# Seven products for eight: the last feed-forward output of a decoder trunk in two recursive units

## The chip, the core and the metric

The kernel runs on one core of a Trainium2 chip. The metric is the device time of one launch in microseconds, as the median of three runs. Times inside an execution come from one profiled execution.

## The reference, cut to what matters

Two layers; each is a feed-forward block, a token mixer and a second feed-forward block on 512 tokens of width 1024. The change touches only the output projection of the very last feed-forward block.

```python
D_MODEL, SEQ, D_FF, DEPTH = 1024, 512, 2816, 2

def swiglu(x, w_in, w_out):
    gate, up = jnp.split(x @ w_in, 2, axis=-1)
    return (jax.nn.silu(gate) * up) @ w_out

for l in range(DEPTH):
    ...
    hn = rms_norm(h, g_ffn2[l]) * (1.0 + sc3) + sh3
    h = h + 0.5 * (1.0 + gt3) * swiglu(hn, w_ffn2_in[l], w_ffn2_out[l])
return h
```

## The kernel before, in words

Everything is held transposed: a tile has 128 features on the partitions and the 512 tokens along the free dimension. The residual stream is `h[0]` to `h[7]`, eight blocks of 128 of the 1024 features; two neighbours share one buffer, so that a listing names them in pairs (`h_85` is blocks 0 and 1, `h_91` blocks 6 and 7). The 2816 inner features of a feed-forward block are 22 blocks, `xs[0]` to `xs[21]`.

Every large float32 product is made from three matmuls. `split` turns an operand into a rounded high part (a cast on ACT, L141: `wH`, `actH`, `comH`) and a low part (a subtraction on DVE, L143: `wL`, `actL`, `comL`); `mm3` (L129 to L131) and `prod` (L433 to L435) then add wH x xH, wH x xL and wL x xH in PSUM. A weight block goes HBM, `wraw` (SP's queue), `wH` and `wL`. The pairs `wH`/`wL` are a ring of four buffers and `wraw` a ring of two, so a cast waits for the matmuls that used the pair four places earlier.

`ffn` works in two groups, `GROUPS = ((0, 12), (12, 22))`. For a group it first makes the inner blocks and then multiplies them by their rows of `w_out` and adds the result, times a gate `cg`, to `h`. The inner blocks are made two at a time by `pair_in`, which already uses a recursion with seven products: `pD`, `pF`, `pG` are PSUM tiles, each product is 24 matmuls of 256 columns (two output blocks, four contraction blocks, three matmuls), and sums of weight blocks are made partly by DMA (`raw` loads a block, `plus` is a second load on POOL's queue that accumulates into it) and partly by DVE (L375). The sums of inputs (`comH`, `comL` with the names P1, P2, T3, T4) are made once by `combine` and serve all pairs. The product with T4 of a pair is put off (`waiting`, `flush`) behind the first products of the next pair.

The output of a group is classical. For each output block i one PSUM tile `ps_mm` collects ten blocks x three matmuls of 512 columns, with the weights of a row in two halves of five blocks (128x640, L304), and `residual` (L343, DVE) adds it to `h[i]`. The last two output blocks, 6 and 7, are done in two halves of the tokens. In the last feed-forward block nothing follows (`ss` is None), so this second group's output, 240 matmuls of 512 columns' worth, is the end of the program; SP then stores each `h[i]` (L1510).

The framework orders the instructions of each engine when the program is built; each engine then works its row off in that order, and a row that waits holds up all rows behind it on its engine.

## Time and profile before

| | |
|---|---|
| median of three runs | 1797.73 us (1796.48 to 1798.9) |
| the profiled execution: time, span | 1801.11 us, 1799.3 us |
| granted TensorE clock | 0.997 |
| PE, DVE, ACT, POOL busy | 98%, 75%, 47%, 8% of the span |
| last pair of inner blocks ends, last output stage begins | 1743.25 us |
| last row of DVE begins | 1795.70 us |

In the rows of the profile the first number is a start in us from the span's beginning, the second the duration; then engine, line, operation, output and inputs, shape; a bracket at the end gives the engine's idle time before the row and what ended it. PEld is the weight load of a matmul; SPq is SP's queue of loads and stores.

### The profile page before, as it was taken

Reading aid. Unit: us, or ns where it says so; the run is one execution under the profiler, and the core shown is the slowest. Engines: PE = TensorE matmul, PEld = TensorE weight load, DVE = VectorE, ACT = ScalarE, POOL = GpSimd, SP = SyncE. Lnnn points to the kernel's source line nnn. Section 1 sums busy time; section 2 is a strip of 40 time slices with the busy share of each in tenths; the row PEclk is TensorE's granted clock in tenths of the full one; section 3 lists DMA queues with packets and bytes.
Section 4 is the critical chain, followed back from the end, with each engine's and each line's share of the span. In section 5 each row is a group of like instructions: output and inputs, shape, how many; then the busy total and the mean of one; then the engine's idle time right before and its main releaser. Section 6 shows DMA issues by size and latency. Waiting matters only on the chain.

```text
span 1799.3 us, 33746 instructions
## 1 busy us (share of the span) xinstructions
PE 1771.5 (98%) x13868; PEld 1616.9 (90%) x13868; DVE 1348.5 (75%) x2175; ACT 844.9 (47%) x1314; POOL 141.4 (8%) x225
## 2 busy tenths in 40 slices
PE   9999999999999999999999999999999999999999
PEld 7898999987778999899899989999876798999998
DVE  7877678777768877677888776887686788865862
ACT  7452355365444554255355515544644345523541
POOL 0101011000000011100100020010000000010000
PEclk9999999999999999999999999999999999999999
DMA  9667877522133676867737697773420427675742
GB/s 378 220 182 260 229 197 214 178 87 79 51 110 103 179 189 219 253 198 203 243 98 203 173 299 195 206 230 102 117 72 28 142 80 205 183 240 135 199 141 71
DMA packets 92267, 309.92 MB, mean 172 GB/s; under 512 B 10512, under 2 KB 11280, under 8 KB 91088
## 3 DMA queue, kind: packets, MB, share of 16 engines
q1 hardware_dynamic: 63072, 202.63, 33.3%
q0 software_dynamic: 29040, 105.13, 23.3%
q8 instruction: 109, 1.79, 0.4%
q14 instruction: 46, 0.38, 0.1%
HBM read 303.79 MB, written 3.93 MB: 171 GB/s over the span
## 4 chain that ended last, share of the span: by engine, by line
PE 84%; DVE 7%; DMA 3%; ACT 3%; issue 3%; POOL 0%; SPq 0%; ACTq 0%; POOLq 0%; DVEq 0%
PE ps_mm L129 14%; PE ps_mm L130 14%; PE ps_mm L131 14%; PE ps_d L433 7%; PE ps_d L435 7%; PE ps_d L434 7%; PE ps_f L435 3%; PE ps_f L433 3%; PE ps_f L434 3%; PE ps_g L435 2%; PE ps_g L433 2%; PE ps_g L434 2%; PE ps_mm L1410 1%; DVE wL L143 1%; DMA wada<-in_wa 1%
## 5 line engine op out<-in xcount | busy, mean ns | idle before, releaser
L141 ACT CAST wH<-wraw 128x1024 fp32r<-128x1024 f32 (+2 forms) x288 | 261.6, 915 | 463.0 <-PE ps_mm L130 198.0
L143 DVE TENSOR_TENSOR wL<-wraw,wH 128x1024 fp32r<-128x1024 f32 (+2 forms) x288 | 303.7, 1058 | 121.5 <-ACT wH L141 120.1
L129 PE MATMUL ps_mm<-actH,wH 128*128 128x512 f32 (+1 forms) x784 | 281.6, 359 | 1.9 <-ACT wH L141 1.9
L131 PE MATMUL ps_mm<-actH,wL 128*128 128x512 f32 (+1 forms) x784 | 281.2, 359 | 0.3 <-DVE wL L143 0.3
L130 PE MATMUL ps_mm<-actL,wH 128*128 128x512 f32 (+1 forms) x784 | 281.0, 358 | 0.0
L129 PE MATMUL ps_mm<-hnH,wH 128*128 128x512 f32 (+1 forms) x712 | 249.6, 356 | 2.9 <-ACT hnH L291 2.6
L130 PE MATMUL ps_mm<-hnL,wH 128*128 128x512 f32 (+1 forms) x712 | 247.1, 349 | 0.3
L131 PE MATMUL ps_mm<-hnH,wL 128*128 128x512 f32 (+1 forms) x712 | 246.1, 347 | 0.6 <-DVE wL L143 0.6
L433 PE MATMUL ps_d<-comH,wH 128*128 128x256 f32 x816 | 225.7, 277 | 0.0
L435 PE MATMUL ps_d<-comH,wL 128*128 128x256 f32 x816 | 224.9, 276 | 0.0
L434 PE MATMUL ps_d<-comL,wH 128*128 128x256 f32 x816 | 224.9, 276 | 0.0
L143 DVE TENSOR_TENSOR wL<-sum,wH 128x1024 fp32r<-128x1024 f32 x102 | 125.0, 1226 | 85.5 <-ACT wH L141 85.4
L199 DVE SCALAR_TENSOR_TENSOR wada<-wada,crep 128x1024 f32<-128x1024 f32 x128 | 153.7, 1222 | 31.5 <-DMA wada<-in_wadaT 31.1
L129 PEld LDWEIGHTS ps_mm<-actH,wH 128*128 128x128 f32 x784 | 149.1, 190 | 18.5 <-ACT wH L141 2.4
L131 PEld LDWEIGHTS ps_mm<-actH,wL 128*128 128x128 f32 x784 | 149.1, 190 | 17.4 <-DVE wL L143 1.1
L130 PEld LDWEIGHTS ps_mm<-actL,wH 128*128 128x128 f32 x784 | 149.1, 190 | 16.2
L433 PEld LDWEIGHTS ps_d<-comH,wH 128*128 128x128 f32 x816 | 157.0, 192 | 1.6 <-ACT s L459 1.6
L435 PEld LDWEIGHTS ps_d<-comH,wL 128*128 128x128 f32 x816 | 157.0, 192 | 0.0
L434 PEld LDWEIGHTS ps_d<-comL,wH 128*128 128x128 f32 x816 | 157.0, 192 | 0.0
L141 ACT CAST wH<-sum 128x1024 fp32r<-128x1024 f32 x102 | 106.9, 1048 | 106.4 <-PE ps_f L434 42.4
L129 PEld LDWEIGHTS ps_mm<-hnH,wH 128*128 128x128 f32 x712 | 135.0, 192 | 23.2 <-issue 7.6
L131 PEld LDWEIGHTS ps_mm<-hnH,wL 128*128 128x128 f32 x712 | 136.6, 192 | 13.7 <-DVE wL L143 1.0
(385 smaller groups left out, 3865.0 us busy)
## 6 DMA issues: line engine op xcount, KB each, us to landing
wada<-in_wadaT POOLq DMA_DIRECT2D x126, 512.0 KB, 4.8
wraw<-in_wmi SPq DMA_DIRECT2D x40, 512.0 KB, 3.5
wraw<-in_w2p SPq DMA_DIRECT2D x36, 512.0 KB, 4.1
wraw<-in_w1p SPq DMA_DIRECT2D x32, 512.0 KB, 4.7
wraw<-in_w1o SPq DMA_DIRECT2D x32, 384.0 KB, 4.9
wraw<-in_w2o SPq DMA_DIRECT2D x32, 384.0 KB, 4.2
wraw<-in_w1o SPq DMA_DIRECT2D x32, 320.0 KB, 3.6
wraw<-in_w2o SPq DMA_DIRECT2D x32, 320.0 KB, 3.4
```

Source lines behind the costliest of these rows:

```text
L129: mm(acc, wH, xH, start=start, stop=False)
L130: mm(acc, wH, xL, start=False, stop=False)
L131: latest["large"] = mm(acc, wL, xH, start=False, stop=stop)
L141: latest["cast"] = nc.scalar.copy(hi, src)
L143: return nc.vector.tensor_sub(lo, src, hi.bitcast(F32))
L199: stt(w, w, 1.0, crep, ALU.mult, ALU.mult, accum_out=out_)
L433: mm(acc, wH, xH, start=start and i + k == 0, stop=False, skip_group_check=True)
L434: mm(acc, wH, xL, start=False, stop=False, skip_group_check=True)
L435: mm(acc, wL, xH, start=False, stop=k == 3, skip_group_check=True)
L1410: latest["large"] = pin("PE", mm(paired(pts[n]), w, x, start=first, stop=last, skip_group_check=True))
```

## The change

In the last feed-forward block, the second group's output goes through a new function `strassen_out`. Eight of its ten inner blocks (12 to 19) are the contraction of a recursion with seven products; blocks 20 and 21 stay classical (`rest_rows`: eight output blocks x two blocks x three matmuls of 512 columns). There are two units, u = 0 and 1, each for four output blocks: g picks two of the four, kh four of the eight contraction blocks. Each unit has seven products of 24 matmuls of 256 columns.

- The sums of inputs P1, P2, T3, T4 are made by `gather` from `actH` and `actL`, four or six steps of 128x512 where `combine` needed two, and split like a weight. P1 is made ahead of unit 0; P2, T3 and T4 between unit 0's products; unit 1 uses them again.
- The sums of weights are made as in `pair_in`, with plain loads and accumulating loads, each now in two pieces of 128x512. Unit 0's first sum `S` takes the buffer `sum0` that the last pair used.
- The products' results reach `h` by `rows_to`, on halves of the tokens.
- The last two blocks of `h` are stored in halves.

```diff
@@ -360,7 +360,7 @@
             com = {n: tuple(ap_.tile([P, 4, H2], F32R, name=x, tag="com", bufs=8) for x in ("comH", "comL")) for n in ("P1", "P2", "T3", "T4")}
             n_first = 2 if first is None else 4
             tiles = (t for t in projector([w_in[l, j, g] for j in range(2 * n_first) for g in range(2)], hn, BANKS[:3], first, 1, ready) if t is not None)
-            xs, waiting, done, after, second = {}, [], [None], [None], [None]
+            xs, Xs, waiting, done, after, second = {}, {}, [], [None], [None], [None]
             def flush():
                 for f in waiting:
@@ -387,6 +387,7 @@
             def new_x(p):
                 X = tuple(ap_.tile([P, 2, T], F32R, name=x, tag="act", bufs=12) for x in ("actH", "actL"))
+                Xs[p] = X
                 for i in range(2):
                     xs[2 * p + i] = tuple(x[:, i] for x in X)
                 return X
@@ -485,6 +486,109 @@
                 waiting.append(rest)
+            def strassen_out(j0, j1):
+
+                kc = j0 + 8
+                full = lambda X, n, sl: X[n][:, :, sl].bitcast(F32)
+                new = {n: tuple(ap_.tile([P, 4, H2], F32R, name=x, tag="com", bufs=8) for x in ("comH", "comL")) for n in ("P1", "P2", "T3", "T4")}
+                q1 = ap_.tile([P, 4, H2], F32, name="q", tag="crep", bufs=1)
+                q2, q3 = (ap_.tile([P, 4, H2], F32, name="q", tag="act", bufs=12) for _ in range(2))
+
+                def gather(name):
+                    for n in range(2):
+                        x1, x2, c = Xs[j0 // 2 + n], Xs[j0 // 2 + 2 + n], slice(2 * n, 2 * n + 2)
+                        if name == "P1":
+                            tt(q1[:, c], full(x1, 0, lo_), full(x1, 0, hi_), ALU.subtract)
+                            tt(q1[:, c], q1[:, c], full(x1, 1, lo_), ALU.add)
+                            tt(q1[:, c], q1[:, c], full(x1, 1, hi_), ALU.subtract)
+                        elif name == "T3":
+                            tt(q3[:, c], full(x2, 0, hi_), full(x1, 0, hi_), ALU.subtract)
+                            tt(q3[:, c], q3[:, c], full(x2, 1, hi_), ALU.add)
+                            tt(q3[:, c], q3[:, c], full(x1, 1, hi_), ALU.subtract)
+                        else:
+                            q, sl = (q1, hi_) if name == "P2" else (q2, lo_)
+                            stt(q2[:, c], q[:, c], -1.0, full(x2, 0, sl), ALU.mult, ALU.subtract)
+                            tt(q2[:, c], q2[:, c], full(x2, 1, sl), ALU.subtract)
+                    split(*new[name], {"P1": q1, "T3": q3}.get(name, q2))
+                    return [tuple(t[:, k] for t in new[name]) for k in range(4)]
+
+                B11, B21, B22 = ([tuple(t[:, sl] for t in xs[k0 + k]) for k in range(4)] for k0, sl in ((j0, lo_), (j0 + 4, lo_), (j0 + 4, hi_)))
+                ncg = small_.tile([P, KD], F32, name="ncg", tag="gmod")
+                ts(ncg, cg, -1.0, None, ALU.mult)
+                flat = lambda t: t.rearrange("p i (b a) -> p i b a", b=2)
+                half_ = lambda n: E(n).rearrange("p (i t) -> p i t", i=2)
+
+                def parts(u, g, kh):
+                    return [(slice(4 * e, 4 * e + 4), w_out[l, 4 * u + 2 * g + e, :, j0 + 4 * kh : j0 + 4 * kh + 4]) for e in range(2)]
+
+                def raw_(srcs, tag=None):
+                    w = (ap_.tile if tag else wp.tile)([P, KD, P], F32, name=tag or "wraw", tag=tag or "wraw", bufs=1 if tag else 2)
+                    for c, s in srcs:
+                        nc.sync.dma_start(w[:, c], s)
+                    return w
+
+                def add_(w, srcs):
+                    for c, s in srcs:
+                        nc.gpsimd.dma_start(w[:, c], s, accum_op=ALU.add)
+
+                def rows_to(i0, gate, sl, x, woven=False):
+
+                    for i in range(2):
+                        hs = h[i0 + i][:, sl]
+                        if woven:
+                            hs = inorder(hs)
+                        stt(hs, x[:, i], gate[:, i0 + i : i0 + i + 1], hs, ALU.mult, ALU.add)
+
+                def rest_rows(u):
+                    w = hl(raw_([(slice(2 * i, 2 * i + 2), w_out[l, 4 * u + i, :, kc:j1]) for i in range(4)]))
+                    for i in range(4):
+                        pt = psum([P, T], "ps_mm", "x")
+                        for k in range(2):
+                            mm3(pt, tuple(t[:, 2 * i : 2 * i + 2] for t in w), k, xs[kc + k], ALL, k == 0, k == 1)
+                        residual(pt, 4 * u + i, cg, None)
+
+                made = {}
+                for u in range(2):
+                    tags = ("mm", "r0", "r1") if u else ("mm", "r1", "r0")
+                    pD, pF, pG = (psum([P, 2, H2], n, t) for n, t in zip(("ps_d", "ps_f", "ps_g"), tags))
+                    vD, vF, vG = (t.rearrange("p i (a b) -> p i b a", b=2) for t in (pD, pF, pG))
+                    up, s1, s2 = half_("up"), half_("s1"), half_("s2")
+                    S = raw_(parts(u, 1, 0), ("sum0", "sum1")[u])
+                    add_(S, parts(u, 1, 1))
+                    a11 = raw_(parts(u, 0, 0), "first")
+                    prod(pD, hl(a11), B11, True)
+                    nc.scalar.copy(flat(s1), vD)
+                    if not u:
+                        made["P1"] = gather("P1")
+                        rest_rows(0)
+                        rest_rows(1)
+                    wS = hl(S)
+                    tt(S, S, a11, ALU.add)
+                    prod(pF, wS, made["P1"], True)
+                    nc.scalar.copy(flat(up), vF)
+                    if not u:
+                        made["P2"] = gather("P2")
+                    prod(pD, hl(S), made["P2"], False)
+                    nc.scalar.copy(flat(s2), vD)
+                    if not u:
+                        made["T3"] = gather("T3")
+                    a12 = raw_(parts(u, 0, 1))
+                    prod(pG, hl(a12, S), B21, True)
+                    tt(flat(s1), vG, flat(s1), ALU.add)
+                    rows_to(4 * u, cg, lo_, s1)
+                    S3 = raw_(parts(u, 0, 0), "third")
+                    add_(S3, parts(u, 1, 0))
+                    prod(pD, hl(S3), made["T3"], False)
+                    tt(flat(up), vD, flat(up), ALU.add)
+                    rows_to(4 * u + 2, ncg, hi_, up)
+                    if not u:
+                        made["T4"] = gather("T4")
+                    prod(pF, hl(S), B22, False)
+                    tt(flat(s2), vF, flat(s2), ALU.add)
+                    rows_to(4 * u, cg, hi_, s2)
+                    prod(pD, hl(raw_(parts(u, 1, 1))), made["T4"], False)
+                    rows_to(4 * u + 2, ncg, lo_, vD, True)
+
             turn_ = [0]
             def pieces(i, g, j0, j1):
@@ -544,6 +648,8 @@
                     cg = small_.tile([P, KD], F32, name="cg", tag="cg")
                     if n_first == 4:
                         ada_until(ap_, crep, l, im + 2)
+                if g and ss is None:
+                    return strassen_out(j0, j1) or []
                 k1 = 0
                 for i in range(KD - 2 * g):
                     if i < 7 - g:
@@ -1507,7 +1613,8 @@
         first = None
         hn = nxt[0] if nxt else None
     for i in range(KD):
-        nc.sync.dma_start(out[i], h[i])
+        for sl in HALVES if i > 5 else (ALL,):
+            nc.sync.dma_start(out[i][:, sl], h[i][:, sl])
 def lay_out(i):
```

How this moves the rows of the engines is shown at three places. The names: `sum_19040` is unit 0's weight sum `S` (buffer `sum0`), `first`, `third` and `wraw` are weight blocks, `q` is a gathered sum, `ps_d`, `ps_f`, `ps_g` are `pD`, `pF`, `pG`.

ACT, from the last pair of inner blocks into the last output stage; before:

```order
L463 COPY s_18887<-ps_d 128x512
L141 CAST wH<-wraw 128x640
L468 ACTIVATE gate<-gate 128x512
L141 CAST wH<-wraw 128x640 x2
L477 ACTIVATE s_18887<-s_18887 128x512
L438 CAST actH<-up 128x2x256
L141 CAST wH<-wraw 128x640
L438 CAST actH<-gate 128x2x256
L141 CAST wH<-wraw 128x640 x12
```

and now:

```order
L464 COPY s_18887<-ps_d 128x512
L141 CAST wH<-first 128x1024
L469 ACTIVATE gate<-gate 128x512
L141 CAST wH<-wraw 128x1024 x2
L478 ACTIVATE s_18887<-s_18887 128x512
L141 CAST wH<-sum_19040 128x1024
L439 CAST actH<-up 128x2x256
L439 CAST actH<-gate 128x2x256
L560 COPY s_19038<-ps_d 128x512
L141 CAST wH<-sum_19040 128x1024
L141 CAST wH<-wraw 128x1024
L141 CAST comH<-q 128x1024
```

The cast of S now stands ahead of the casts of the last inner blocks, `actH`.

DVE in the last output stage; before, only weight splits and residuals:

```order
L143 TENSOR_TENSOR wL<-wraw,wH 128x640 x4
L343 SCALAR_TENSOR_TENSOR h_87<-ps_mm,cg,h_87 128x512
L143 TENSOR_TENSOR wL<-wraw,wH 128x640 x3
L343 SCALAR_TENSOR_TENSOR h_87<-ps_mm,cg,h_87 128x512
L143 TENSOR_TENSOR wL<-wraw,wH 128x640 x2
```

and now, in unit 0, from the sum with a12 over T3's split to T4's split:

```order
L375 TENSOR_TENSOR sum_19040<-sum_19040,wraw 128x1024
L143 TENSOR_TENSOR wL<-third,wH 128x1024
L143 TENSOR_TENSOR comL<-q,comH 128x1024
L577 TENSOR_TENSOR s_19038<-ps_g,s_19038 128x512
L510 SCALAR_TENSOR_TENSOR q<-q,actH 128x512
L540 SCALAR_TENSOR_TENSOR h_85<-s_19038,cg,h_85 128x256 x2
L511 TENSOR_TENSOR q<-q,actL 128x512
L510 SCALAR_TENSOR_TENSOR q<-q,actH 128x512
L582 TENSOR_TENSOR up<-ps_d,up 128x512
L540 SCALAR_TENSOR_TENSOR h_87<-up,ncg,h_87 128x256 x2
L143 TENSOR_TENSOR wL<-sum_19040,wH 128x1024
L143 TENSOR_TENSOR comL<-q,comH 128x1024
```

Gather steps, residuals and splits for three products alternate in one row.

PE at the end of T3's product of unit 0, now (before, the matmuls of L129 to L131 stand here without a break); 19034, 19035 are unit 0's `pD` and `pF`, 19381 and 19382 unit 1's, and com 19027 is T4:

```order
L434 MATMUL ps_d_19034<-comH_19025,wH_19280 128x256
L435 MATMUL ps_d_19034<-comL_19026,wH_19280 128x256
L436 MATMUL ps_d_19034<-comH_19025,wL_19281 128x256
L434 MATMUL ps_d_19381<-actH_17859,wH_19395 128x256 [waits Activation_49]
L435 MATMUL ps_d_19381<-actL_17860,wH_19395 128x256
L434 MATMUL ps_f_19382<-comH_19021,wH_19424 128x256 [waits Activation_49]
L435 MATMUL ps_f_19382<-comL_19022,wH_19424 128x256
L434 MATMUL ps_d_19034<-comH_19027,wH_19351 128x256 [waits Activation_49]
L436 MATMUL ps_f_19035<-actH_18292,wL_19318 128x256 [waits DVE_49]
L434 MATMUL ps_f_19035<-actH_18292,wH_19317 128x256
```

The first matmuls of unit 1 and of T4's product stand ahead of the rest of B22's product (`pF` of unit 0).

## The prediction

> **What bounds the kernel now.** I read the page first: busy time, then the chain that ended last.

> ```profile
> PE 1771.5 (98%) x13868; PEld 1616.9 (90%) x13868; DVE 1348.5 (75%) x2175; ACT 844.9 (47%) x1314; POOL 141.4 (8%) x225
> PE 84%; DVE 7%; DMA 3%; ACT 3%; issue 3%; POOL 0%; SPq 0%; ACTq 0%; POOLq 0%; DVEq 0%
> ```

> PE carries the span. Next I asked for the last stretches of the windows view, since the change touches only the last 55 us (columns: stretch and its length, then PE, PEld, DVE, ACT and POOL busy, PEclk, DMA share, GB/s).

> ```profile
> 1740.00:1760.00 20.00, 20.00 (x109) 17.98 (x108) 10.25 (x14) 7.44 (x11) 0.00 (x0) 1.00 0.41 129
> 1760.00:1780.00 20.00, 20.00 (x95) 17.57 (x94) 7.93 (x10) 4.41 (x7) 0.00 (x0) 1.00 0.25 79
> ```

> In the stage that changes PE never waits, while DVE works half the time and ACT a third. Fewer matmuls are therefore time saved, as long as DVE and ACT keep up with what replaces them. The timeline shows the stage's borders, its output rows on DVE, and the last store:

> ```profile
> 1743.14 0.28 PE L435 MATMUL ps_d<-comH,wL 128*128 128x256 f32 x1
> 1743.25 0.38 PE L129 MATMUL ps_mm<-actH,wH 128*128 128x512 f32 x1
> ...
> 1775.83 0.75 DVE L343 SCALAR_TENSOR_TENSOR h<-ps_mm,cg,h 128x512 f32<-128x512 f32 x1 [4.13 <-PE ps_mm L131]
> 1782.30 0.75 DVE L343 SCALAR_TENSOR_TENSOR h<-ps_mm,cg,h 128x512 f32<-128x512 f32 x1 [5.72 <-PE ps_mm L131]
> 1785.65 0.48 DVE L343 SCALAR_TENSOR_TENSOR h<-ps_mm,cg,h 128x256 f32<-128x256 f32 x1 [2.60 <-PE ps_mm L131]
> 1789.00 0.48 DVE L343 SCALAR_TENSOR_TENSOR h<-ps_mm,cg,h 128x256 f32<-128x256 f32 x1 [2.87 <-PE ps_mm L131]
> ...
> 1795.39 0.28 PE L131 MATMUL ps_mm<-actH,wL 128*128 128x256 f32 x1
> 1795.70 0.48 DVE L343 SCALAR_TENSOR_TENSOR h<-ps_mm,cg,h 128x256 f32<-128x256 f32 x1 [2.87 <-PE ps_mm L131]
> ```

> One output row is 30 matmuls: 1782.30 - 1775.83 = 6.47 us at 512 columns, 0.2158 each; 1789.00 - 1785.65 = 3.35 us at 256, 0.1117 each. All times below are on this profile's clock.

> **The change: matmuls.** Before: 6 x 30 of 512 and 4 x 30 of 256, from 1743.25 to 1795.50 (last start plus one pitch), 52.25 us. After: 14 products of 24 at 256 columns, 336 x 0.1117 = 37.53, and 48 of 512 for the two classical blocks, 48 x 0.2158 = 10.36; together 47.89. **Saved: 4.36 us.** This leans on weight loads staying covered at 256 columns, because there are now 384 of them where there were 300:

> ```profile
> L131 PEld LDWEIGHTS ps_mm<-actH,wL 128*128 128x128 f32 x784 | 149.1, 190 | 17.4 <-DVE wL L143 1.1
> ```

> A load of 190 ns fits under a pitch of 112 ns only because loads overlap matmuls; the two rows of 256 columns above show that they do. [...]

> **The change: what PE now waits for.** DVE and ACT prices come from back-to-back rows of the last full pair, and from the same combinations on the input side:

> ```profile
> 1708.08 0.68 DVE L439 TENSOR_TENSOR actL<-up,actH 128x512 fp32r<-128x512 f32 x1
> 1708.68 1.22 DVE L375 TENSOR_TENSOR sum<-sum,wraw 128x1024 f32<-128x1024 f32 x1
> 1709.82 1.22 DVE L143 TENSOR_TENSOR wL<-third,wH 128x1024 fp32r<-128x1024 f32 x1
> ...
> 1727.30 1.05 ACT L141 CAST wH<-third 128x1024 fp32r<-128x1024 f32 x1 [0.63 <-ACT up L455]
> 1728.25 0.58 ACT L459 COPY s<-ps_d 128x512 f32<-128x512 f32 x1
> ...
> L416 DVE SCALAR_TENSOR_TENSOR q<-x,q x8: 684/686/692, 83.0 to 1495.9; 128x512 f32<-128x512 f32 x8
> ```

> So DVE starts a new operation 0.60 us after one of 512 elements and 1.14 after one of 1024 (0.69 and 1.22 to its end); a gather step is a 512 one. ACT: 0.95 after a cast of 1024, 1.05 to its end. DVE rows of 256 I take at 0.40 to the next start, below their 0.48.

> *P1 gather.* Its six steps stand in two earlier pairs, three at a time (3 x 0.60), ahead of the split of a weight sum:

> ```profile
> 1715.59 1.22 DVE L143 TENSOR_TENSOR wL<-sum,wH 128x1024 fp32r<-128x1024 f32 x1 [1.50 <-ACT wH L141]
> ```

> DVE sat idle 1.50 before such a split, so 0.4 us sticks out, and that sum is first used by the next pair's first product, behind two whole products of this one (2 x 24 x 0.1117 = 5.4 us): nothing. Without that cover it would be 0.4 us twice. P1's own split (0.95 ACT, 1.14 DVE) lies in the pair before the end, where DVE has 15.06 of 20 us busy:

> ```profile
> 1720.00:1740.00 20.00, 20.00 (x181) 20.00 (x180) 15.06 (x17) 10.63 (x15) 0.00 (x0) 1.00 0.52 154
> ```

> Nothing again, except that the last split of the old sum, S of the last pair, ends some 0.45 later.

> *Unit 0's first sum (wait 1).* S of unit 0 takes the buffer sum0 of the last pair, which is free when this ends:

> ```profile
> 1731.02 1.23 DVE L143 TENSOR_TENSOR wL<-sum,wH 128x1024 fp32r<-128x1024 f32 x1 [0.27 <-ACT wH L141]
> ...
> sum<-in_w2p SPq DMA_DIRECT2D x1, 512.0 KB, 3.5
> third<-in_w2p POOLq DMA_DIRECT2D x1, 512.0 KB, 5.4
> sum<-in_w2p POOLq DMA_DIRECT2D x1, 512.0 KB, 8.0
> ```

> That is 1732.7 with the 0.45. The load lands 3.5 to 4 us later, at 1736.5; behind it POOL issues the accumulating load, after that of third. In the pair at 1694 to 1708, whose DMA rows stand above, an accumulating load took 5.4 us, and 8.0 behind another. I take 7.7, nearer the second: S is there at **1744.2**; bounds 1742 (5.4) to 1747 (8.0 and POOL's extra issues, since each load now comes in two pieces). [...]

> On ACT and DVE the split of S stands ahead of the casts of the last pair's actH and actL, which the classical blocks read. ACT: S 1744.2, actH(up) 1745.15, actH(gate) 1745.67 to 1746.29. DVE: wL of S 1745.28, actL(up) 1746.42, actL(gate) 1747.02 to 1747.71. PE ends the last pair at 1743.25 and the first product at 1745.93; it waits 0.43 for actH, does 0.66 of work, and waits 0.77 for actL: **1.2 us**. Were S early, the floor is 0.4, since its weight pair takes a ring buffer that the last pair frees only at 1743.3. Each us that S is later than 1743.4 costs one. The two banks of the classical rows add about 0.2, one gather step or split standing between residuals.

> *Unit 0's T3 (wait 2).* After the last classical residual starts on DVE, at 1758.97, there stand 0.66 + four gather steps 2.4 + split of a12 1.14 + a step 0.6 + sum 1.14 + split of third 1.14 + split of T3 1.22 = 8.3 us. PE meanwhile has 18 matmuls of F, P2's and G's product, (18 + 24 + 24) x 0.1117 = 7.4 us, and then must have T3: with the handovers **1.2 us**.

> *Unit 0's T4 (wait 3).* PE's row then has the first matmuls of unit 1 and of T4 ahead of the rest of B22's product. Unit 1's S needs the ring buffer that T3's product frees at its end, so its cast runs 1.05 with PE idle but for 0.22: 0.98. T4's cast stands behind it on ACT, and its last gather step behind the residual work on DVE: 1.48 more. Then B22's wL, behind two residual rows: 0.75. **3.2 us.**

> In unit 1 nothing is gathered; its split of the second sum costs 0.07. Sum of waits: 1.2 + 0.2 + 1.2 + 3.2 + 0.1 = 5.9, PE's last matmul 5.9 - 4.36 = **1.6 us later**.

> *End.* Two residual rows follow the last product, where one did: 0.40 more.

> ```profile
> 1792.86 3.68 SPq L1510 DMA_DIRECT2D out<-h  x2
> L1510 SPq DMA_DIRECT2D out<-h x8: 332/338/344, 1750.7 to 1796.2; - x8
> DMA to landing us min/median/max: 2.0/2.0/2.6
> ```

> The last store is issued as DVE ends (1796.2 now) and the span ends 3.1 later. Halves hide the first of the two last stores' issue (0.34) under the second row (0.40), so nothing more.

> **Sum: +2.0 us.** The profiled execution had a span of 1799.3 and a time of 1801.11, 3.4 above the median of 1797.73; the span would be 1801.3, and I put the same 2.0 on the median: **1799.7 us**. A measurement of this kernel can tell some 0.2%, 3.6 us, so this is within that bound.

> **The rivals.** *S comes late* (slower): from 1745.8 on wait 1 alone takes the sum beyond 3.6. S at 1747 gives 1802.5, and the classical weights behind it in the same queues would add up to 1 more. For it: 8.0 for an accumulating load behind another, and four DMA issues where two were; against it: fewer plain loads run beside it than at 1700. Chance 0.26. *The gathers hide* (faster): if DVE and ACT are ahead where I have them last, waits 2 and 3 vanish and only wait 1's floor and the end remain: 0.4 + 0.4 - 4.4 = -3.6, 1794.1; with half of the waits left, 1796.3. For it: DVE is busy 75% overall, and my 8.3 against 7.4 is close; against it: wait 3 hangs on ring buffers that only PE's own progress frees. Chance 0.10. *Weight loads stand alone*: 84 more x 0.19 = 16 us on top, 1815.7; the 256-column rows speak against it. Chance 0.01. The forecast has 0.63.

> **How the numbers follow.** Costs within the forecast: DVE starts 3% quicker or slower move the gathers by 0.7 to 1.0 either way; S between 1742 and 1745.5 moves -0.8 to +1.3. So its own range is 1797.9 to 1801.3. The range for 8 in 10 reaches halfway into both rivals: 1796.0 to 1803.5. Faster by over 0.2% (below 1794.1) needs all gathers hidden: 0.06. Slower by over 0.2% (above 1801.3) is the late S, the weight loads and a little of the forecast: 0.28. The rest, 0.66, is within 0.2%.

> **What would show it.** Right: PE without a wait up to 1743; then some 1.2 us idle before the second and third classical matmul, released by ACT actH and DVE actL; 1.2 before T3's product; three waits of about 1, 1.5 and 0.7 before the rest of B22's, the last two released by comH and wL; unit 1 solid. DVE nearly full from 1758 to 1776. Wrong: an accumulating load of sum that lands before 1743.4 or after 1746; waits 2 and 3 together under 2 us; a pitch of 256-column matmuls other than 0.112; waits in unit 1; or any wait in the pairs in which P1 is gathered.

## The result, and the profile after

Over seven runs the changed kernel took 1806.57 us in the median (1799.53 to 1807.57), the kernel before 1797.73 (1795.89 to 1801.5): a ratio of 1.0042, 95% interval 1.0027 to 1.0058. By the ratio it is slower by 7.6 us where 2.0 was forecast.

The profiled execution took 1805.48 us. Its page:

```profile
PE 1770.9 (98%) x13952; PEld 1617.4 (90%) x13952; DVE 1384.9 (77%) x2224; ACT 856.2 (47%) x1324; POOL 148.3 (8%) x233
PE 85%; DVE 8%; ACT 3%; DMA 3%; issue 1%; SPq 0%; POOL 0%; DVEq 0%; ACTq 0%; POOLq 0%
```

The view of the cores (span, mean granted clock; before had 0.997):

```profile
core 0: 1803.7 us, clock 0.995
```

PE is as busy as it was, although it has less to do. The windows view of the stage (columns as in the prediction) says why:

```profile
1740.00:1760.00 20.00, 16.94 (x89) 14.83 (x88) 16.29 (x22) 7.61 (x10) 0.00 (x0) 0.91 0.37 100
1760.00:1780.00 20.00, 16.90 (x129) 16.10 (x128) 19.05 (x26) 7.71 (x9) 1.72 (x2) 0.91 0.44 105
```

Two things stand where before had 20.00 and a clock of 1.00: PE waits 3.1 us in each stretch, and its clock is granted at 0.91. The timeline of PE has the waits:

```profile
1740.57 0.28 PE L434 MATMUL ps_d<-actH,wH 128*128 128x256 f32 x1
...
1743.14 0.28 PE L436 MATMUL ps_d<-actH,wL 128*128 128x256 f32 x1
1745.97 0.70 PE L129 MATMUL ps_mm<-actH,wH 128*128 128x512 f32 x2 [2.56 <-ACT actH L439]
...
1747.39 0.48 PE L130 MATMUL ps_mm<-actL,wH 128*128 128x512 f32 x1 [0.50 <-DVE actL L440]
...
1748.15 0.62 PE L130 MATMUL ps_mm<-actL,wH 128*128 128x512 f32 x1
...
1766.92 0.28 PE L434 MATMUL ps_d<-comH,wH 128*128 128x256 f32 x1
...
1768.24 0.38 PE L435 MATMUL ps_d<-comL,wH 128*128 128x256 f32 x1 [0.70 <-DVE comL L143]
1768.45 0.28 PE L436 MATMUL ps_d<-comH,wL 128*128 128x256 f32 x1
...
1771.02 0.28 PE L435 MATMUL ps_d<-actL,wH 128*128 128x256 f32 x1
1772.10 0.38 PE L434 MATMUL ps_f<-comH,wH 128*128 128x256 f32 x1 [0.80 <-ACT wH L141]
1772.31 0.28 PE L435 MATMUL ps_f<-comL,wH 128*128 128x256 f32 x1
1773.71 0.38 PE L434 MATMUL ps_d<-comH,wH 128*128 128x256 f32 x1 [1.13 <-ACT comH L141]
1774.56 0.38 PE L436 MATMUL ps_f<-actH,wL 128*128 128x256 f32 x1 [0.47 <-DVE wL L143]
1774.77 0.28 PE L434 MATMUL ps_f<-actH,wH 128*128 128x256 f32 x1
```

They are the forecast's three waits, at the forecast's places, with its releasers. In two places the clock is also halved for some 3.4 us, a slow stretch from here on. Windows of that length show it (PEclk is the third from the end):

```profile
1748.20:1751.60 3.40, 3.40 (x10) 2.77 (x9) 2.46 (x5) 1.05 (x1) 0.00 (x0) 0.51 0.49 154
1751.60:1755.00 3.40, 3.40 (x17) 2.97 (x17) 3.16 (x6) 0.93 (x1) 0.00 (x0) 1.00 0.00 0
1772.20:1775.60 3.40, 1.80 (x11) 1.42 (x12) 3.40 (x6) 1.04 (x1) 1.68 (x2) 0.98 0.53 72
1775.60:1779.00 3.40, 3.40 (x19) 3.40 (x18) 2.45 (x4) 0.00 (x0) 0.00 (x0) 0.52 0.73 131
```

From the stage's first matmul to the span's end before had 1799.3 - 1743.25 = 56.05 us, after 1803.7 - 1740.57 = 63.13: 7.1 more. In parts: matmuls -4.36; wait 1 3.6 (from 1743.25 to 1748.15 are 4.90, with five matmuls of 512 columns and two of 256 in them, 1.30); wait 2 1.1 (1766.92 to 1768.45 less four pitches); wait 3 3.2 (1771.02 to 1774.77 less five); the clock 3.4 (twice 3.41 us at half); the end 0.3. Sum 7.2.

Why was wait 1 three times its size? The timelines of ACT, SP and POOL before it:

```profile
1735.30 1.05 ACT L141 CAST wH<-wraw 128x1024 fp32r<-128x1024 f32 x1 [1.10 <-PE ps_d L435]
1740.65 1.05 ACT L141 CAST wH<-wraw 128x1024 fp32r<-128x1024 f32 x1 [4.31 <-PE ps_d L435]
1741.61 0.63 ACT L478 ACTIVATE s<-s 128x512 f32<-128x512 f32 x1
1743.84 1.04 ACT L141 CAST wH<-sum 128x1024 fp32r<-128x1024 f32 x1 [1.60 <-DMA sum<-in_w2o]
1744.79 0.61 ACT L439 CAST actH<-up 128x512 fp32r<-128x512 f32 x1
...
1730.01 0.80 SPq L527 DMA_DIRECT2D sum<-in_w2o  x2
1734.33 1.72 POOL L532 DMA_DIRECT2D sum<-in_w2o  x2 [0.59 <-DMA sum<-in_w2o]
```

The DMA view of the same time (KB each, median us from issue to landing):

```profile
wraw<-in_w2o SPq DMA_DIRECT2D x8, 128.0 KB, 4.5
sum<-in_w2o POOLq DMA_DIRECT2D x2, 256.0 KB, 8.0
```

ACT stood still for the accumulating load of S until 1743.84. It had already stood still 4.31 us ahead of the cast of the second classical weights, the last four of the eight loads of 128 KB, and the SiLU of the last pair had to wait behind that cast: its input was there at 1738.78, and it started at 1741.61. The bracket puts this wait down to PE. In early sum and in both kernels without gathers, below, the same cast waits for `DMA wraw` (4.20, 4.83 and 3.88 us), so it is the load that counts. Which of the two, S or these weights, keeps PE waiting had to be tried.

### The profile page after: what moved, and what is told of

It is laid out like the page before. It is cut to its first block, busy times and chain, and to the rows that moved or that the text cites. A ratio compares the mean times of both kernels' runs of the same rounds, so it can differ in the third digit from the quotient of the medians.

```text
span 1803.7 us, 34019 instructions
## 1 busy us (share of the span) xinstructions
PE 1770.9 (98%) x13952; PEld 1617.4 (90%) x13952; DVE 1384.9 (77%) x2224; ACT 856.2 (47%) x1324; POOL 148.3 (8%) x233
## 4 chain that ended last, share of the span: by engine, by line
PE 85%; DVE 8%; ACT 3%; DMA 3%; issue 1%; SPq 0%; POOL 0%; DVEq 0%; ACTq 0%; POOLq 0%
PE ps_mm L129 14%; PE ps_mm L130 14%; PE ps_mm L131 14%; PE ps_d L434 7%; PE ps_d L436 7%; PE ps_d L435 7%; PE ps_f L436 4%; PE ps_f L434 3%; PE ps_f L435 3%; PE ps_mm L1516 2%; PE ps_g L434 2%; PE ps_g L436 2%; PE ps_g L435 2%; DVE wL L143 2%; ACT wH L141 1%
## 5 line engine op out<-in xcount | busy, mean ns | idle before, releaser
L141 ACT CAST wH<-wraw 128x1024 fp32r<-128x1024 f32 (+2 forms) x278 | 256.4, 929 | 454.7 <-PE ps_mm L130 197.3
L143 DVE TENSOR_TENSOR wL<-wraw,wH 128x1024 fp32r<-128x1024 f32 (+2 forms) x278 | 297.2, 1073 | 115.0 <-ACT wH L141 113.6
L129 PE MATMUL ps_mm<-actH,wH 128*128 128x512 f32 (+1 forms) x700 | 253.8, 363 | 2.6 <-ACT actH L439 2.6
L130 PE MATMUL ps_mm<-actL,wH 128*128 128x512 f32 (+1 forms) x700 | 253.7, 362 | 0.5 <-DVE actL L440 0.5
L131 PE MATMUL ps_mm<-actH,wL 128*128 128x512 f32 (+1 forms) x700 | 253.7, 362 | 0.3 <-DVE wL L143 0.3
L129 PE MATMUL ps_mm<-hnH,wH 128*128 128x512 f32 (+1 forms) x712 | 248.6, 354 | 2.9 <-ACT hnH L291 2.6
L131 PE MATMUL ps_mm<-hnH,wL 128*128 128x512 f32 (+1 forms) x712 | 245.5, 346 | 0.6 <-DVE wL L143 0.6
L434 PE MATMUL ps_d<-comH,wH 128*128 128x256 f32 x864 | 238.5, 276 | 1.2 <-ACT comH L141 1.1
L435 PE MATMUL ps_d<-comL,wH 128*128 128x256 f32 x864 | 237.8, 275 | 0.7 <-DVE comL L143 0.7
L436 PE MATMUL ps_d<-comH,wL 128*128 128x256 f32 x864 | 237.6, 275 | 0.0
L143 DVE TENSOR_TENSOR wL<-sum,wH 128x1024 fp32r<-128x1024 f32 x108 | 132.2, 1224 | 80.0 <-ACT wH L141 79.9
L141 ACT CAST wH<-sum 128x1024 fp32r<-128x1024 f32 x108 | 113.1, 1047 | 120.0 <-PE ps_f L435 39.2
L435 PEld LDWEIGHTS ps_d<-comL,wH 128*128 128x128 f32 x864 | 166.0, 192 | 0.9 <-DVE comL L143 0.9
L129 PEld LDWEIGHTS ps_mm<-hnH,wH 128*128 128x128 f32 x712 | 134.4, 191 | 23.4 <-issue 7.6
L129 PEld LDWEIGHTS ps_mm<-actH,wH 128*128 128x128 f32 x700 | 132.9, 190 | 18.4 <-ACT actH L439 2.8
L131 PEld LDWEIGHTS ps_mm<-hnH,wL 128*128 128x128 f32 x712 | 136.1, 191 | 13.9 <-DVE wL L143 1.0
L130 PEld LDWEIGHTS ps_mm<-hnL,wH 128*128 128x128 f32 x712 | 136.1, 191 | 13.0 <-DVE hnL L292 1.0
L131 PEld LDWEIGHTS ps_mm<-actH,wL 128*128 128x128 f32 x700 | 133.1, 190 | 16.3 <-DVE wL L143 0.7
## 6 DMA issues: line engine op xcount, KB each, us to landing
wada<-in_wadaT POOLq DMA_DIRECT2D x126, 512.0 KB, 4.7
wraw<-in_wmi SPq DMA_DIRECT2D x40, 512.0 KB, 3.5
wraw<-in_w2p SPq DMA_DIRECT2D x36, 512.0 KB, 4.5
wraw<-in_w1p SPq DMA_DIRECT2D x32, 512.0 KB, 4.5
sum<-in_w2p SPq DMA_DIRECT2D x18, 512.0 KB, 4.3
```

The costliest lines, as they stand in the source:

```text
L129: mm(acc, wH, xH, start=start, stop=False)
L130: mm(acc, wH, xL, start=False, stop=False)
L131: latest["large"] = mm(acc, wL, xH, start=False, stop=stop)
L141: latest["cast"] = nc.scalar.copy(hi, src)
L143: return nc.vector.tensor_sub(lo, src, hi.bitcast(F32))
L434: mm(acc, wH, xH, start=start and i + k == 0, stop=False, skip_group_check=True)
```

## The experiments

Each experiment shared its chip with runs of the kernel before, 21 to 35 of them in each of four groups. Where a kernel computes other numbers, its expectation says so.

| kernel | median, us | against before, 95% | mean clock |
|---|---|---|---|
| before (116 runs, medians of four groups) | 1796.6 to 1798.8 | | 0.998 |
| the change | 1806.57 | 1.0027 to 1.0058 | 0.995 |
| early sum | 1802.57 | 1.0019 to 1.0040 | 0.997 |
| no gather | 1798.64 | 1.0003 to 1.0020 | 0.997 |
| early sum, no gather | 1798.61 | 0.9992 to 1.0010 | 0.998 |
| filled wait | 1804.43 | 1.0023 to 1.0045 | 0.997 |
| no gather, filled | 1799.78 | 1.0002 to 1.0025 | 0.998 |
| rows between | 1798.32 | 1.0000 to 1.0018 | 0.998 |
| early gather | 1798.47 | 0.9988 to 1.0007 | 0.997 |
| all early | 1796.03 | 0.9982 to 0.9999 | 0.998 |
| before, idle by four | 1803.95 | 1.0028 to 1.0057 | 0.997 |
| before, idle by one | 1800.09 | 1.0012 to 1.0031 | 0.998 |
| early spread | 1795.09 | 0.9982 to 1.0002 | 0.998 |
| early sum, one weight | 1796.15 | 0.9987 to 1.0006 | 0.998 |
| spread behind two rows | 1795.24 | 0.9975 to 0.9993 | 0.998 |
| spread behind one row | 1794.77 | 0.9976 to 0.9994 | 0.999 |

**Early sum.** Unit 0's S takes the buffer that is free a pair earlier.

```diff
-S = raw_(parts(u, 1, 0), ("sum0", "sum1")[u])
+S = raw_(parts(u, 1, 0), ("sum1", "sum0")[u])
```

> Only the buffers of the two units' first weight sums are exchanged: unit 0 takes sum1, free since the pair before the last, and unit 1 takes sum0. Theory (three terms were missed or mis-sized: the sum S of unit 0 lands late, PE then sits idle, and idle time is followed by some 3.4 us at half the granted clock): S is there before the last pair ends, so the 3.6 us lost around the first classical matmuls fall to about 0.4, and the first stretch at half clock (1.7 us) goes; the waits before T3's and T4's products and the stretch behind them stay. Time about 1801.5 us, some 5 below the changed kernel. Rival (the loss lies in the seven products' extra work on DVE and ACT alone): within 1.5 us of the changed kernel's 1806.6.

Part came back, but wait 1 did not go. ACT and PE in its timelines:

```profile
1741.27 1.05 ACT L141 CAST wH<-wraw 128x1024 fp32r<-128x1024 f32 x1 [4.20 <-DMA wraw<-in_w2o]
1742.22 0.63 ACT L478 ACTIVATE s<-s 128x512 f32<-128x512 f32 x1
...
1745.53 0.70 PE L129 MATMUL ps_mm<-actH,wH 128*128 128x512 f32 x2 [1.39 <-ACT actH L439]
1747.16 0.80 PE L130 MATMUL ps_mm<-actL,wH 128*128 128x512 f32 x1 [0.71 <-DVE actL L440]
```

S no longer counts; the cast of the second classical weights does, and SiLU and actH behind it. The slow stretch behind the wait stayed as well.

**No gather; early sum and no gather.** P2, T3 and T4 read P1's sums; the second kernel has the early sum too.

```diff
-made["P2"] = gather("P2")
+made["P2"] = made["P1"]
```

> The gathered sums P2, T3 and T4 are left out: their products use the split of P1 instead (part of the computation is replaced, 14 DVE steps of 512 elements, three splits and three casts less). Theory: the waits before T3's and T4's products (1.1 and 3.2 us) and the stretch at half clock behind them (1.7) go, the late S and its stretch stay: about 1800.6 us. Rival (those waits are weight buffers, not gathers): the wait of unit 1's first cast for the ring, 1 us, and most of the loss stay, 1804 or more.

> Both of the others at once (gathers of P2, T3 and T4 left out, sums exchanged). Theory: what is left is the count of matmuls, 4.4 us less than the classical form, against 0.4 us of wait and 0.3 at the end: about 1794 us, faster than the kernel before, clock as before it. Rival (the recursive form loses more than the waits show, for example to weight loads at 256 columns or to its DMA): 1797 us or more.

Without the gathers waits 2 and 3 and the second slow stretch are gone, and wait 1 is all that PE's timeline shows:

```profile
1744.65 0.58 PE L129 MATMUL ps_mm<-actH,wH 128*128 128x512 f32 x1 [2.55 <-ACT actH L439]
```

So waits 2 and 3 come with the gathers. (PE's row loses the first matmuls of unit 1 ahead of B22's product too; how much of wait 3 hung on that order is not told apart.) With the early sum on top, wait 1 still had 1.08 + 0.71, so the floor of 0.4 was missed again, and so was the expected 1794: five of its eleven executions took 1794.1 to 1795.7 at clocks of 0.998 to 1.000, six 1798.6 to 1800.5 at 0.994 to 0.997. The profiled one, 1794.35, has no slow stretch in the stage; where the six have theirs is not seen.

**One load of classical weights.** This tests what the two runs above suggested: the early sum, and the second classical weights left out.

```diff
+if not u:
+    made["rest"] = hl(raw_(...))
+w = made["rest"]
-w = hl(raw_(...))
```

> The kernel with the early sum (unit 0's S in sum1), and no second load of classical weights: the lower four rows' two classical blocks use the weights of the upper four (other numbers come out; 512 KB less to load, one cast and one split less). Theory A (with S early, what keeps wait 1 alive is the cast of these second weights, which stands ahead of the SiLU on ACT and waits for its transfer): wait 1 falls from 2.1 in the kernel with the early sum to 0.4 or less, and its half-clock stretch goes; waits 2 and 3 and their stretch stay: 1802.6 - 1.7 - 1.7 = 1799.2. Theory B (wait 1 is the length of the chain add, SiLU, multiply, cast itself): 1.5 us or more stay, with the stretch, 1802.

```profile
1742.75 0.70 PE L129 MATMUL ps_mm<-actH,wH 128*128 128x512 f32 x2 [0.34 <-ACT actH L439]
```

Wait 1 is 0.34, below the floor, and its slow stretch is gone. So wait 1 had two causes, the late S and the late second weights, both of them transfers that stand ahead of the last pair's SiLU or casts on ACT. (With the second weights their cast and split go too; that the transfer is what counts rests on the brackets.) The time fell by more than expected, 6 us against the early sum by the two ratios, since waits 2 and 3 shrank too (0.62, 0.83 and two of 0.20) and had no slow stretch behind them.

**Idle time in the kernel before.** The clock's part, by itself: nothing of the change, only PE held up at 1743.25.

```diff
+z = E("z")[:, :1]
+ts(z, last_pd[0][:, 1, :1], 0.0, None, ALU.mult)
+for _ in range(4):
+    act(xs[j0][0], xs[j0][0].bitcast(F32), AF.Identity, bias=z)
```

> The kernel before, with idle time for TensorE put in by hand at the place where the change begins: behind the last pair's last product DVE makes a column of zeros from its bank, and ACT adds that zero four times to the first block that the classical rows read (its numbers stay as they are). Nothing else moves: PE has the same 300 matmuls in the same order. By the rows of before, PE stands still from 1743.25 until gate (0.25 + 0.69), the zeros (0.3) and four ACT operations (4 x 0.55) are done: 3.8 us. Theory A (after a window that is mostly idle the clock is granted at half for 3.4 us, which costs 1.7): 3.8 + 1.7 = 5.5 us over before's median, 1803; the profile shows one stretch of half-clock rows behind the idle time. Theory B (the stretches in the changed kernel belong to its own products, not to idle time): +3.8, 1801.3, no such rows.

> As before with idle time put in by hand, with one ACT operation where there were four: PE idle for about 2.1 us. Theory A, if the clock falls only when most of a window of 3.4 us is idle: the 2.1 us alone, 1799.6, and no half-clock rows in most runs; if 2.1 us of idle time are enough, 3.8 over before, 1801.3. Theory B: +2.1, 1799.6.

The first one's wait in PE's timeline, and then its windows (PEclk third from the end):

```profile
1749.27 0.80 PE L129 MATMUL ps_mm<-actH,wH 128*128 128x512 f32 x1 [5.07 <-ACT actH L554]
```

```profile
1744.20:1749.20 5.00, 0.01 (x1) 0.00 (x0) 2.72 (x5) 4.12 (x7) 0.00 (x0) 0.97 0.41 124
1749.20:1752.60 3.40, 3.33 (x8) 2.71 (x9) 0.00 (x0) 0.02 (x1) 0.00 (x0) 0.54 0.02 5
1752.60:1756.00 3.40, 3.40 (x17) 2.99 (x16) 0.83 (x1) 0.73 (x1) 0.00 (x0) 1.00 0.00 0
```

The wait came out longer than planned, 5.07, and 5.07 + 1.7 = 6.8 was to be expected by theory A; +7.4 was measured (5.0 to 10.2 by the interval). The time alone does not exclude theory B's 5.1; the profile decides, since the same matmuls that ran at full clock in before run for 3.4 us at half clock here. With one operation the wait was 2.81; its profile has no slow stretch in the stage, and the median is 3.5 up. Seven of its runs lie at 1798.2 to 1800.4, with clocks of 0.998 and 0.999, and five at 1801.0 to 1804.3, with 0.995 to 0.998; which of these five had their slow stretch here is not seen, as one execution was profiled.

**Filling the wait.** Twelve matmuls of 512 columns behind unit 0's first product, in the changed kernel and in the one without gathers.

```diff
+for n in range(12):
+    mm(spare_bank, ones_r, xs[j0][0], start=n == 0, stop=n == 11)
```

> The changed kernel with 12 matmuls of 512 columns more on PE, whose result nobody reads, behind unit 0's first product, where PE waits for the late S (12 x 0.216 = 2.6 us of work in a wait of 3.6). Theory of the clock: the wait is as long as before, but PE is busy in it, so the granted clock stays at 1.00 there and the 1.7 us at half clock go: about 1804.9 us in executions that had the stretch. Rival (the clock falls for another reason, such as the mix of products or temperature): the stretch near 1748 stays and the time is 1806.6 or more.

> No gathers but P1's (P2, T3 and T4 read P1's sums, so the outputs are other numbers), and 12 idle-time matmuls of 512 columns behind unit 0's first product, which write a bank that is overwritten later; the order on DVE and ACT is that of the kernel without gathers and without the 12. In that kernel's profile PE lost 2.55 us at wait 1 and then ran a 3.4 us stretch at half the granted clock. Theory A (the clock follows the idle time): the 12 take 12 x 0.2158 = 2.59 us, so the wait is filled and nothing is later than it was; the profile shows no row of half clock in this stage, which is 1.7 us shorter, and the median is 1.7 below the 1798.64 of the kernel without the 12: 1796.9, at a mean granted clock of about 0.998. Theory B (the clock falls at that place for a reason of its own, such as the load of the first fast rows): the half-clock stretch stays, the median stays at 1798.6 or is later by up to 0.5.

Neither is clean. In the first, four gather steps and a split came to stand ahead of the first residual on DVE: PE waited 2.14 us for it, and the slow stretch moved behind that wait. In the second the classical weights came later still, so waits of 0.83, 1.15 and 1.49 followed the filled one, and the median did not fall. What the second does show: 3.5 us of idle time within 7 us, in three pieces with 0.48 and 2.64 us of work between, left the clock at 1.00.

**Rows between; early gather; all early.** Towards a version that keeps the saving. In all three S is early and the classical rows stand behind unit 0's second and fourth product; the second and third add gather steps in earlier pairs.

```diff
-made["P1"] = gather("P1"); rest_rows(0); rest_rows(1)
+made["P1"] = gather("P1")
 prod(pF, wS, made["P1"], True)
+if not u: rest_rows(0)
...
 prod(pG, hl(a12, S), B21, True)
+if not u: rest_rows(1)
```

> The sums swapped (unit 0's S in sum1, free a pair earlier), and the two classical rows' blocks moved: one behind unit 0's second product, one behind its fourth (G), so that neither the casts of the last pair's actH and actL nor the rest rows' weights are awaited right after the last pair, and 5.2 us of classical matmuls lie ahead of P2's product and 5.2 ahead of T3's. Theory A (waits 1, 2, 3 are lateness that other work can cover, and the clock falls only after idle time): wait 1 is 0.4 at most, wait 2 gone, of wait 3 the 1.0 of the ring buffer and up to 1.0 of T4's gather stay; no half-clock stretch after wait 1, one of 1.7 us after wait 3 possible. 1797.5 - 4.4 + 0.4 + 2.0 + 0.4 = 1795.9, up to 1797.6 with a stretch. Theory B (DVE is the bound of unit 0: the same gathers, splits and residuals have to be done before T4's product, wherever the rows lie): the waits only gather at T3 and T4, 4 to 5 us in all, with a stretch of half clock: 1799 to 1801.

> As the kernel with the rows between, and the gathers' additions moved forward: P1's in the program ahead of the pair before the last, P2's ahead of the last pair, T3's behind it; only T4's stay. DVE has 5 us idle in each of these pairs. Theory A: waits 1 to 3 fall to 0.5 to 1.5 us in all, the four steps of P2 in the last pair cost at most 0.7 there; no half-clock stretch: 1797.5 - 4.4 + 1.0 + 0.4 + 0.4 = 1794.9, between 1794 and 1796.5, so faster than before. Theory B (the steps in the last pair delay what PE waits for there as much as they save behind): 1797.5 to 1799, with waits before the last pair's T3 product or B22 product.

> As the kernel with early gathers, but T3's additions stand with P2's ahead of the last pair: ten steps in a row on DVE, 6.1 us, behind the last pair's first row of DVE work, ahead of the gate of the pair before and of the split of third. Theory A (DVE has slack of about 5 us in that pair and PE is 2 products behind): PE waits 1 to 2 us in the last pair before T3's product, less than 0.5 behind it: 1795 to 1796. Theory B (the ten steps hit the split of third and the sum in the last pair in full): 3 to 4 us of wait in the last pair and a half-clock stretch there: 1798 to 1800.

The first came at 1798.32, between the two theories: wait 1 is gone, the first wait is 0.47 for a residual, the others are 0.2 to 0.6 each, and there is no slow stretch in the stage. In the second, actH came 2.17 us late, a slow stretch followed, and nothing was gained. The third is faster than before, just (0.01 to 0.18%): it pays in the last pair,

```profile
1732.94 0.38 PE L434 MATMUL ps_f<-hnH,wH 128*128 128x256 f32 x1 [0.81 <-ACT wH L141]
```

and later only 0.43, with no slow stretch.

**Spread.** P1's and P2's steps early, T3's behind the last pair's splits, then behind two residual rows, or one.

```diff
+rested = residual(pt, 4 * u + i, cg, None)
+if u == 0 and i == 1:          # the other kernel: i == 0
+    with tc.issue_after(rested.ins):
+        adds(j0, "T3")
```

> Sums swapped, the two classical rows' blocks behind unit 0's second and fourth product, gathers early as in the early kernel, but T3's additions spread behind the last pair's last splits instead of ahead of its gate (where the early kernel lost 2.17 us) and not in a row of ten ahead of the split of third (where the kernel with all early lost 0.98). Theory A: waits below 0.6 us in all, no half-clock rows: 1797.7 - 4.4 + 0.6 + 0.4 + 0.3 = 1794.6. Theory B (DVE, now without a pause, sets the pace, and every step moved turns up as a wait somewhere else): 1796 or more.

> As the kernel with the early, spread gathers (1795.1, where PE still lost 1.43 us because four steps of T3 and a split stood ahead of the first residual on DVE), with T3's six steps held back until two residual rows are done. Theory A (what the matmul count saves is there once the waits and, with them, the half-clock stretches are gone): less than 0.5 us of waits in the stage, no half-clock rows, 1797.0 - 4.4 + 0.4 (tail) + 0.5 = 1793.5, faster than before by 0.2%. Theory B (DVE has no idle time from 1727 to 1775, so a step that moves away from one wait makes another): the 1.4 us turn up at the next residual, at P2 or at T3: 1795.

> The same with T3's six steps behind the first residual row. Theory A: the second residual now stands behind six steps, 3.6 us, and with it the bank for the fourth row: up to 1.5 us of wait in the first four classical rows or at P2's product, 1795. Theory B: as for its neighbour, 1795.

All three come to about 1795. For the first the interval still holds 1; the last two are faster than before, by 0.15% (0.06 to 0.25). In each of them one wait of 1.3 to 1.4 us moves to another residual: theory B. The windows of the last one, beside those of the result above:

```profile
1740.00:1760.00 20.00, 18.45 (x117) 16.59 (x117) 20.00 (x28) 9.22 (x11) 0.59 (x2) 1.00 0.35 111
1760.00:1780.00 20.00, 20.00 (x180) 19.97 (x179) 18.04 (x23) 8.72 (x10) 1.14 (x2) 1.00 0.39 106
```

DVE is full for 20 us, which points to the gathers as what now holds back the rest; no run in this order has fewer of them, so that is argued and not shown. Of the 4.4 us that the matmul count saves, 2.7 arrive by the ratio (1.1 to 4.5 by the intervals).

## Why the prediction was wrong

*The saving* (4.36) is right: the first product's rows go from 1740.57 to 1743.14 in 23 pitches, 0.1117 each, and the last two kernels keep 2.7 of it (1.1 to 4.5). *Weights that stand alone* did not occur: the loads of that product took 192 ns each (PEld), more than its pitch of 112. *P1's gather* cost nothing, as said: PE's rows from 1710 to the stage's begin show no wait.

*Wait 1* is the first step that failed. The forecast took S as there at 1744.2 on before's clock, "7.7, nearer the second" of two accumulating loads. The stage began 2.7 us earlier in this execution, so its plain load was issued where I had it (1730.01 is 1732.7 on that clock) but S arrived at 1743.84, or 1746.5: 9.5 us behind POOL's issue at 1734.33. Each us costs one by the forecast's rule, so 1.2 becomes 3.5, and 3.6 were measured. The DMA engines had no room there, at a share of 1.05. The windows view of after, its last columns the DMA share and GB/s:

```profile
1735.00:1740.00 5.00, 5.00 (x47) 5.00 (x46) 2.61 (x3) 1.05 (x1) 1.05 (x2) 1.00 1.05 208
```

and of before, on its own clock:

```profile
1735.00:1740.00 5.00, 5.00 (x47) 5.00 (x46) 2.99 (x4) 2.10 (x3) 0.00 (x0) 1.00 0.75 213
```

The same GB/s take a share of 1.05 instead of 0.75. By the DMA view of these 5 us, 0.58 of the 1.04 MB were accumulating loads and took 0.725; the plain loads, 0.45 MB, took 0.324, per MB about as much as before's 1.06 MB with 0.747. I had argued that "fewer plain loads run beside it". They did not thin out: from POOL's issue to the arrival of S (1734.3 to 1743.9) there were 1.00 MB of them, 0.10 MB per us, and in the pair with the row of 8.0 us (before, 1698.8 to 1706.9) 0.82 MB, 0.10 too. So the row of 8.0 was the one under the same load, and 7.7 was too short; I put the rest down to the two pieces and to POOL's issue, 0.5 us behind my 1736.5; no run takes these shares apart. By its own terms this is the rival *S comes late*, which decides from 1745.8 on, at a chance of 0.26; its price, 1802.5 to 1803.5, has no loss of clock in it either. And "the floor is 0.4" was wrong with S early: the cast of the second classical weights, which I had ready in time, held wait 1 at 1.8 to 2.1 until that load was taken out (0.34).

*Wait 2* (1.2) measured 1.1. *Wait 3* (3.2) measured 3.2 in the forecast's order: by the starts, less one pitch each, its three waits are 0.97, 1.29 and 0.74, where 0.98, 1.48 and 0.75 were forecast. *Unit 1* was solid, *the end* 0.3 for 0.4. The 0.2 for the banks of the classical rows and the 0.1 in unit 1 did not occur.

*The clock* is the second step: it is not in the sum at all. Every row I read of this stage had 1.00, with PE never waiting there, and I left it at 1.00 for a stage to which I was adding 6 us of waits. Two slow stretches cost 3.4.

With both steps mended the forecast's sum is 2.0 + 2.4 + 3.4 = 7.8, and 7.5 without the two small terms that did not occur; measured were 7.1 in the profiled execution and 7.6 by the ratio. The one run at 1799.53 doesn't speak for the forecast: its clock was 0.999, and 43 of before's 116 runs with that clock have a median of 1795.8.

## What to carry over

Price each wait that a change adds to a solid stretch of TensorE together with the clock behind it: in the profiles of this stage 3.4 us in which TensorE was busy for 0.52 or less were followed eight times by 3.4 us at half clock, 1.7 us lost each time where matmuls stood ready; behind one wait of 2.81 us the clock stayed at 1.00. The change lost twice. Before trusting a saving in matmuls, follow what stands ahead of the critical operation in each engine's order: one weight cast ahead of a SiLU kept the stage waiting after its supposed cause was gone. And take the time of a load from a row under the same load (8.0 us here, not the 5.4 of the one ahead of it), or keep its whole range.

## What the runs showed of the hardware

The kernel before has slow stretches too. Its profiled execution has a slow stretch in three windows of ten us, none of them near the stage; ahead of the last one PE's timeline has an idle time of 2.29 us:

```profile
351.00:361.00 10.00, 9.76 (x69) 9.44 (x70) 6.90 (x23) 4.16 (x10) 0.00 (x0) 0.83 0.20 63
571.00:581.00 10.00, 9.13 (x67) 8.88 (x66) 7.71 (x19) 3.96 (x10) 0.00 (x0) 0.83 0.36 105
1371.00:1381.00 10.00, 7.71 (x89) 4.38 (x87) 9.48 (x20) 0.83 (x1) 0.00 (x0) 0.83 0.27 81
```

```profile
1375.52 0.30 PE L663 MATMUL ps_t<-TT,X 64*64 64x64 f32 x5 [2.29 <-DVE X L1000]
```

The other kernels' profiles, with the same code up to the last pairs, have such stretches at some of the same places (near 350, 490, 570, 1230 and 1375, and in early sum one each from 900 to 1100 and from 1100 to 1300), from four of them (early sum) down to none (spread behind one row). Before's 116 runs go with the mean clock: 1793.7 to 1794.2 at a clock of 1.000, a median of 1795.8 at 0.999, 1798.4 to 1801.0 at 0.996.

The traces' records of the clock show how the stretches are placed. In the profiles of before and of the change each is 3413 ns long, except the one behind PE's last matmul, with which the record ends (1727 and 2959 ns), and the starts within an execution lie whole multiples of 3413.3 ns apart: 65, 235 and 124 of them in before, 163, 195, 149, 8 and 8 in the changed kernel. In the other profiles the six slow stretches of the last stage come to 3.40 to 3.44 us by windows of 1 and 2 us, and the two of early sum begin 27.3 us apart as well.

Each of the eight slow stretches of the last stage follows 3.4 us in which PE was busy for 0.00 to 0.52 of the time. Laid on windows of 3413.3 ns that run through before's slow stretches, the wait of 2.29 us lies in one that was busy for 0.33, and a slow stretch followed; around and behind the wait of 2.81 us, in the kernel idle by one, PEclk is 1.00 from 1738.80 to 1748.40. How that wait lies to such windows is not seen, so why one wait was followed by a slow stretch and the other not is not shown. In before and the changed kernel together, from where the record begins (7.6 and 7.4 us), each of the 3 windows busy for less than 0.45 was followed by a slow stretch, 5 of the 15 busy for 0.45 to 0.70 were, and so were 2 of the busier ones (0.82 and 0.84, both ahead of a stretch at 574). No sharp border can be read from that, and the ends of matmuls are modelled in the profile.
